# A two-layer decoder trunk on one core: smaller first weight load, norm sums closed before the operands, attention steps regrouped

## The chip, the cores and the metric

The kernel runs on one core of a Trainium2 chip. The metric is device time in microseconds (us) of one execution; three executions of the kernel before were timed, and one more was profiled. Engines: TensorE multiplies matrices (PE in the rows, PEld for its weight loads), VectorE (DVE) does two-operand arithmetic, ScalarE (ACT) functions and copies, GpSimd (POOL) almost nothing here, SyncE (SP) issues every load and store.

## The reference

Two layers over x of 256 positions x 1024 features, all float32. With adaLN columns shift, scale and gate made from c for each sub-layer, every sub-layer does x <- x + gate * f(rmsnorm(x) * (1 + scale) + shift):

```python
def reference(x, c, ...):
    sc = jax.nn.silu(c)
    for i in range(DEPTH):                      # DEPTH = 2
        mod = sc @ w_ada[i] + b_ada[i]
        sh_m, sc_m, g_m, sh_f, sc_f, g_f = jnp.split(mod, 6, axis=-1)
        h = modulate(x, norm_mix[i], sh_m, sc_m)
        y = moba_attention(h, ...) if i % 2 == 0 else short_conv(h, ...)
        x = x + g_m[:, None, :] * y
        h = modulate(x, norm_ffn[i], sh_f, sc_f)
        x = x + g_f[:, None, :] * swiglu(h, w_gate_up[i], w_down[i])
    return x
```

Layer 0 is attention with 8 heads of 128 features, RMS norm on q and k per head; with 256 positions there is one block of 256 keys, so it is plain causal attention. Layer 1 is a gated convolution of width 3. The channel mixer is SwiGLU with 2816 features.

## The kernel before, in words

**Numbers.** float32 products are made from two-part operands: a tile is split into a rounded part (`..h`, float32r) and the rest (`..l`), and `mm3` (line 250) issues three matmuls of 256 columns: high by high, high by low, low by high. The split costs one ScalarE copy and one VectorE subtraction for every tile (`prep` for weights, lines 91 to 100, each weight tile in two halves; `split` and others for activations).

**Order.** Up to the end of the first products (line 546 on, `manual_schedule`) TensorE, VectorE and ScalarE follow the written order. Behind it a scheduler lays out each engine's queue when the program is built: from the written order as priority, raised inside `high_priority(400)`, and from its own estimates of when an instruction could start. Once laid out, each engine takes its queue in order. SyncE's loads go in the written order. Weight tiles and the rows of the adaLN matrix share five buffers (`wf`), the split weights three (`wh`, `wl`); a load is issued when its buffer is free.

**Start (lines 546 to 621).** SyncE loads columns, x, the first adaLN pieces and `first_rows(0)`, the first 128 rows of the q and half of the k weights: 1536 columns, loaded as 1024 and then 512. The first norm's row factors are made, x is turned by TensorE, and for row block k = 0 to 7 the loop at line 594 makes the scale column (VectorE, `scale_column`), splits the weights (`w_operands` the first two of six 256-column pieces, `operands` the rest), makes the operand of the activations (`normed`, `h_operand`: `m0h` by ScalarE, `m0l` by VectorE) and issues `first_products`, six column tiles of six matmuls. For k = 0 all this stands above the loop: `shift_columns(y, 0)` (line 587), then `turn_x`, then `w_operands(0, wf)` (line 589), then `operands`. `keep_warm` issues matmuls whose result nobody reads.

**Attention (lines 624 to 762).** `tok_gemm` for the last two k tiles and four v tiles is the stream numbered g = 0 to 5, each of eight blocks k of six matmuls; g = 6 is the first group of `out_proj`, eight blocks of twelve. `plan[g, k]` names steps issued ahead of block k: `turn(j)` turns two k heads on TensorE and copies them out; `softmax(h)` makes the scores of head h, their maximum, exponential and normalisation; `turn_probs(h)` turns the probabilities; `mix_values(h)` multiplies them with v and splits the result into `ov` (line 725). In block k of g = 6 the output products read `ov[k]`. The plan of before places the four turns and the eight calls of each other step in four lists (lines 739 to 746).

**Norms (class `Norm`, lines 314 to 363).** `out_proj` finishes feature tiles of x in groups ([0, 1], [2], [3] of 256 features for the output projections, one each for the down projections), then for every tile of 128 calls `residual` (VectorE) and `done`. For the norms n0, n1, n2 `done` is `take(k)`: it squares the tile (ScalarE), adds the square to the running sum (VectorE; the last square is kept apart as `self.last`) and makes the two parts of the operand x * scale (`rh` by ScalarE, `rl` by VectorE). `raw_gemm` then starts the next matrix on x * scale without the row factor; at block k = 2 `rstd` (line 345) makes the mean square of each row by products of the sum, and of the last square, with the column `inv_d`, and at k = 4 `rows` turns the factors into a row tile. The result is multiplied by it at the end. In the last down projection `done` is `store`.

Of the kernel before, what the change touches and what calls it, by code (L numbers as in the profile page):

```python
# [33 lines left out]
def trunk_kernel(ctx: ExitStack, tc: tile.TileContext, x_t, cols_in, scale_in, shift_in, ada_in, qk_rows, kv_in, o_in,  # L34
# [99 lines left out]
    def first_rows(k):  # L134
        wf = wpool.tile([P, 8, CW], F32, tag="wf", name=f"wf_qk_{k}", bufs=5)
        flat = wf.rearrange("p k c -> p (k c)")
        for cs in (slice(0, D), slice(D, D + D // 2)):
            nc.sync.dma_start(flat[:, cs], qk_rows[k][:, cs])
        return wf

# [173 lines left out]
    class Norm:  # L314
# [2 lines left out]
        def __init__(self, name, l, sh, scl, raw):  # L317
            self.name, self.n, self.l, self.sh, self.scl, self.raw = name, 0, l, sh, scl, raw

        def take(self, k):  # L320
            sq = tmp.tile([P, S], F32, tag="sq", name=f"sq_{self.name}_{k}", bufs=2)
            nc.scalar.activation(sq, xT[:, k], AF.Square)
            if self.n == 0:
                self.sum = sq
            elif self.n == 1:
                s = tmp.tile([P, S], F32, tag="ssum", name=f"ss_{self.name}_{k}", bufs=1)
                nc.vector.tensor_add(s, self.sum, sq)
                self.sum = s
            elif self.n < KD - 1:
                nc.vector.tensor_add(self.sum, self.sum, sq)  # L330
            else:
                self.last = sq
            self.n += 1
            rh, rl = self.raw
            a = mcol(self.l, self.scl, k)
            nc.scalar.activation(rh[:, k, :S], xT[:, k], AF.Copy, scale=a)
            nc.vector.scalar_tensor_tensor(rl[:, k, :S], xT[:, k], a, rh[:, k, :S].bitcast(F32), op0=ALU.mult,
                                           op1=ALU.subtract)
            if k == (4 if self.sh == SH_F else 0):
                i = self.l * 48 + self.sh * KD  # L340
                sh = mod[:, i:i + KD].unsqueeze(2).to_broadcast([P, KD, 2])
                nc.scalar.activation(rh[:, :, S:], sh, AF.Copy)
                nc.vector.tensor_sub(rl[:, :, S:], sh, rh[:, :, S:].bitcast(F32))

        def rstd(self):
            ps = ps_misc("ms_" + self.name)
            for t in range(2):
                ts = slice(t * P, (t + 1) * P)
                nc.tensor.matmul(ps[:, t:t + 1], self.sum[:, ts], inv_d, start=True, stop=False)
                nc.tensor.matmul(ps[:, t:t + 1], self.last[:, ts], inv_d, start=False, stop=True)  # L350
            sd = tmp.tile([P, 2], F32, tag="sd", name="sd_" + self.name)
            r = tmp.tile([P, 2], F32, tag="rs", name="rs_" + self.name)
            with tc.high_priority(400):
                nc.scalar.activation(sd, ps[:, :2], AF.Sqrt, bias=eps)
                nc.vector.reciprocal(r, sd)
            self.r = r
# [8 lines left out]
    def residual(ps, l, gate, k):  # L365
        nc.vector.scalar_tensor_tensor(xT[:, k], ps, mcol(l, gate, k), xT[:, k], op0=ALU.mult, op1=ALU.add)

    def out_proj(keys, xs, l, gate, done, between={}):
        groups = [[0, 1], [2], [3]] if len(keys[0]) == 1 else [[j] for j in range(4)]
        for js in groups:  # L370
# [18 lines left out]
                        base + k == 0, base + k == total - 1)  # L389
                base += nk  # L390
            with tc.high_priority(400):
                for (j, o), ps in pss.items():
                    residual(ps, l, gate, 2 * j + o)
                    done(2 * j + o)

    def split(dst, k, src, name, psum_src=False):
        nc.scalar.activation(dst[0][:, k], src, AF.Copy)
# [133 lines left out]
    def keep_warm(n):  # L531

        ps = ps_misc("warm")
        for _ in range(n):
            nc.tensor.matmul(ps[:, :2 * P].rearrange("p (n c) -> p n c", c=P), ident_r,
                             ident_r.unsqueeze(1).to_broadcast([P, 2, P]), start=True, stop=True, skip_group_check=True)
# [9 lines left out]
    with tc.manual_schedule(engines={mybir.EngineType.PE, mybir.EngineType.DVE, mybir.EngineType.Activation}):  # L546
# [37 lines left out]
        t = normed(0)  # L584
        nc.vector.tensor_copy(xT[:, 2:4], x_ps)
        keep_warm(2)
        shift_columns(y, 0)
        x_ps = [turn_x(i, ps_alt) for i in (2, 3)]
        ops = w_operands(0, wf)
        operands(0, t, wf, ops)  # L590
        for i in range(2):
            nc.scalar.activation(xT[:, 4 + 2 * i:6 + 2 * i], x_ps[i], AF.Copy)
# [143 lines left out]
    for j in range(2):  # L736
        to_features(j, accs[4 + j])
    plan = {}
    for n, (g, k) in enumerate([[0, 4], [2, 4], [3, 1], [3, 7]]):
        plan.setdefault((g, k), []).append((turn, n))  # L740
    for n, (g, k) in enumerate([[3, 0], [3, 3], [3, 4], [4, 5], [5, 2], [5, 7], [6, 2], [6, 6]]):
        plan.setdefault((g, k), []).append((turn_probs, n))
    for n, (g, k) in enumerate([[2, 2], [2, 7], [3, 1], [3, 6], [4, 3], [5, 0], [5, 4], [5, 7]]):
        plan.setdefault((g, k), []).append((softmax, n))
    for n, (g, k) in enumerate([[3, 5], [3, 7], [4, 6], [5, 0], [5, 6], [6, 1], [6, 3], [6, 7]]):
        plan.setdefault((g, k), []).append((mix_values, n))

    def between(g):
        return {k: plan[g, k] for k in range(KD) if (g, k) in plan}
# [9 lines left out]

    av = new_pair("a", "a0", KF)  # L760
    n0 = Norm("n0", 0, SH_F, SC_F, raw_in(av))
    out_proj([[(("o", j), KD)] for j in range(4)], ov, 0, G_M, n0.take, between(6))
    zv, zraw = wide_pair("zv")
    n1 = Norm("n1", 1, SH_M, SC_M, zraw)
    ffn(0, n0, av, n1.take)


    ups = [act.tile([P, 2, S + 2], F32, tag=f"up{i}", name=f"up{i}") for i in range(2)]
# [33 lines left out]

    av = new_pair("a", "a1", KF)
    n2 = Norm("n2", 1, SH_F, SC_F, raw_in(av))
    out_proj([[(("co", j), KD)] for j in range(4)], zv, 1, G_M, n2.take)


    def store(k):
# [2 lines left out]
        elif k % 2:  # L811
            nc.sync.dma_start(out_f[:, k - 1:k + 1], xT[:, k - 1:k + 1])

    ffn(1, n2, av, store)


def _lay_out(inputs):
# [57 lines left out]
```

## Time and profile before

| | us |
|---|---|
| timed, median of 3 (lowest to highest) | 589.35 (589.28 to 589.84) |
| the profiled execution | 591.96 |
| its span, first to last instruction | 590.2 |
| TensorE busy in the span | 581.8 |
| VectorE busy | 453.3 |
| ScalarE busy | 315.1 |

Busy time of an engine says how much it did and not what the end waited for. A TensorE record is longer than the time that it takes from the next one, since matmuls overlap; the distance between two starts is the cost. A bracket behind a row of the timeline is idle time of that engine ahead of the instruction and what ended it. The chain that ended last is followed back from the last instruction, at each step to what released it.

### The profile page before, as it was taken

To read this page: it belongs to the slowest core of one execution; us is meant where nothing else is said; L and a number is where in the kernel's file an instruction comes from. 1 tells how busy PE (TensorE), PEld (TensorE's weight loads), DVE (VectorE), ACT (ScalarE), POOL (GpSimd) and SP (SyncE) were. 2 spreads that over 40 slices of the span, in tenths; PEclk is the share of its full clock that TensorE was granted. 3 is DMA by queue.
4 is the path that set the end of the run, shared out by engine and by line. 5 is a ranking of instruction groups with operands and counts; after the bars stand their busy time and mean duration, and the time that the engine had idled before them with its cause. 6 is when DMAs were issued, how large, how long until landed. Compare 5 with 4: busy or idle time off the path is not lost.

```text
span 590.2 us, 12039 instructions
## 1 busy us (share of the span) xinstructions
PE 581.8 (99%) x5044; PEld 573.0 (97%) x5044; DVE 453.3 (77%) x719; ACT 315.1 (53%) x526; POOL 1.1 (0%) x8
## 2 busy tenths in 40 slices
PE   8999999999999999999999999999999999999997
PEld 7999999999999999999999999999999999999997
DVE  4789898998989777868788999758976576565550
ACT  6457789596644353543337655446854454443330
POOL 0000000000000000000000000000000000000000
PEclk9999999999999999999999999999999999999999
DMA  8999998945898889768988279746386575655400
GB/s 322 396 378 406 354 330 318 349 159 205 323 344 329 325 314 355 261 219 330 338 339 300 87 284 366 267 143 230 132 351 243 190 284 189 242 183 191 160 18 18
DMA packets 25109, 156.04 MB, mean 264 GB/s; under 512 B 2784, under 2 KB 3168, under 8 KB 8928
## 3 DMA queue, kind: packets, MB, share of 16 engines
q1 hardware_dynamic: 25056, 155.28, 71.0%
q8 instruction: 39, 0.64, 0.4%
q14 instruction: 14, 0.11, 0.0%
HBM read 154.22 MB, written 1.05 MB: 263 GB/s over the span
## 4 chain that ended last, share of the span: by engine, by line
PE 86%; DMA 5%; DVE 5%; ACT 2%; issue 1%; SPq 0%; DVEq 0%; ACTq 0%
PE pu L252 7%; PE pu L253 7%; PE pu L256 7%; PE pg L252 6%; PE pg L256 6%; PE pg L253 6%; DMA wa<-in_ada_dram 4%; PE op_d L256 4%; PE op_d L253 4%; PE op_d L252 4%; PE pq L252 1%; PE pq L253 1%; PE op_o L252 1%; PE raw_f L252 1%; DVE prod L109 1%
## 5 line engine op out<-in xcount | busy, mean ns | idle before, releaser
L109 DVE SCALAR_TENSOR_TENSOR prod<-wa,c_all 128x1024 f32<-128x1024 f32 x80 | 97.7, 1221 | 26.9 <-DMA wa<-in_ada_dram 26.0
L99 DVE TENSOR_TENSOR wl_d<-wf_d,wh_d 128x1024 fp32r<-128x1024 f32 (+1 forms) x48 | 52.9, 1132 | 23.7 <-ACT wh_d L98 23.7
L98 ACT ACTIVATE wh_d<-wf_d 128x1024 fp32r<-128x1024 f32 (+1 forms) x48 | 44.8, 979 | 44.5 <-PE op_d L253 22.3
L98 ACT ACTIVATE wh_g<-wf_g 128x1024 fp32r<-128x1024 f32 x44 | 45.8, 1052 | 41.9 <-issue 41.7
L99 DVE TENSOR_TENSOR wl_u<-wf_u,wh_u 128x1024 fp32r<-128x1024 f32 x44 | 52.3, 1220 | 13.3 <-ACT wh_u L98 13.1
L98 ACT ACTIVATE wh_u<-wf_u 128x1024 fp32r<-128x1024 f32 x44 | 44.6, 1050 | 32.7 <-issue 27.1
L99 DVE TENSOR_TENSOR wl_g<-wf_g,wh_g 128x1024 fp32r<-128x1024 f32 x44 | 53.4, 1221 | 1.7 <-ACT wh_g L98 1.6
L256 PE MATMUL op_d<-a0h,wl_d 128*128 128x256 f32 x176 | 49.1, 279 | 1.1 <-DVE wl_d L99 1.1
L252 PE MATMUL op_d<-a0h,wh_d 128*128 128x256 f32 x176 | 48.8, 277 | 0.0
L253 PE MATMUL op_d<-a0l,wh_d 128*128 128x256 f32 x176 | 48.8, 277 | 0.0
L252 PE MATMUL op_d<-a1h,wh_d 128*128 128x256 f32 x176 | 48.6, 276 | 0.0
L253 PE MATMUL op_d<-a1l,wh_d 128*128 128x256 f32 x176 | 48.6, 276 | 0.0
L256 PE MATMUL op_d<-a1h,wl_d 128*128 128x256 f32 x176 | 48.6, 276 | 0.0
L252 PE MATMUL pg<-f0h,wh_g 128*128 128x256 f32 x160 | 44.5, 278 | 0.0
L256 PE MATMUL pg<-f0h,wl_g 128*128 128x256 f32 (+3 forms) x164 | 44.4, 275 | 0.0
L252 PE MATMUL pg<-f1h,wh_g 128*128 128x256 f32 x160 | 44.2, 277 | 0.0
L253 PE MATMUL pg<-f0l,wh_g 128*128 128x256 f32 x160 | 44.2, 276 | 0.0
L252 PE MATMUL pu<-f0h,wh_u 128*128 128x256 f32 x160 | 44.2, 276 | 0.0
L253 PE MATMUL pu<-f0l,wh_u 128*128 128x256 f32 x160 | 44.2, 276 | 0.0
L256 PE MATMUL pu<-f0h,wl_u 128*128 128x256 f32 x160 | 44.2, 276 | 0.0
L253 PE MATMUL pg<-f1l,wh_g 128*128 128x256 f32 x160 | 44.2, 276 | 0.0
L256 PE MATMUL pg<-f1h,wl_g 128*128 128x256 f32 x160 | 44.2, 276 | 0.0
(296 smaller groups left out, 2027.6 us busy)
## 6 DMA issues: line engine op xcount, KB each, us to landing
wa<-in_ada_dram SPq DMA_DIRECT2D x40, 1024.0 KB, 6.0
wf_g<-in_gate_up_dram SPq DMA_DIRECT2D x22, 1024.0 KB, 5.1
wf_u<-in_gate_up_dram SPq DMA_DIRECT2D x22, 1024.0 KB, 5.0
wf_d<-in_down_dram SPq DMA_DIRECT2D x16, 1024.0 KB, 6.9
wf_d<-in_down_dram SPq DMA_DIRECT2D x8, 768.0 KB, 4.9
wa_sc<-in_scale_dram SPq DMA_DIRECT2D x8, 512.0 KB, 6.6
wa_sh<-in_shift_dram SPq DMA_DIRECT2D x8, 512.0 KB, 7.5
wf_qk<-in_qk_rows_dram SPq DMA_DIRECT2D x8, 512.0 KB, 6.4
```

What stands on the lines that cost most here:

```text
L98: nc.scalar.activation(wh[:, a:b], wf[:, a:b], AF.Copy)
L99: nc.vector.tensor_sub(wl[:, a:b], wf[:, a:b], wh[:, a:b].bitcast(F32))
L109: nc.vector.scalar_tensor_tensor(t, w, 1.0, c_all, op0=ALU.mult, op1=ALU.mult, accum_out=dst)
L252: nc.tensor.matmul(ps, ah, bh, start=first, stop=False, skip_group_check=True)
L253: nc.tensor.matmul(ps, ah, bl, start=False, stop=False, skip_group_check=True)
L256: nc.tensor.matmul(ps[:, a:b], al, bh[:, a:b], start=False, stop=last, skip_group_check=True)
```

## The change

1. `first_rows`: the first row block's weights are loaded as 512 and then 1024 columns; the other seven as before. `w_operands(0, wf)`, the split of the first 512 columns, is written ahead of `shift_columns(y, 0)`.
2. `Norm.take` becomes `square` and `operand`. The last square is added to the sum as well, and `rstd` makes two products with `inv_d` where it made four. `out_proj` calls, for each tile of x, residual, square, operand as before; in the group of the last tiles it makes both residuals, then both squares, then both operands. The stores of the last projection come behind both residuals in the same way.
3. The plan of attention has eleven stops and the first `turn`. At stop i stand, where they exist, `mix_values(i - 3)`, `turn_probs(i - 2)`, `turn(i + 1)` and `softmax(i)`.

```diff
--- before.py
+++ after.py
@@ -134,7 +134,9 @@
     def first_rows(k):
         wf = wpool.tile([P, 8, CW], F32, tag="wf", name=f"wf_qk_{k}", bufs=5)
         flat = wf.rearrange("p k c -> p (k c)")
-        for cs in (slice(0, D), slice(D, D + D // 2)):
+
+        n = D if k else D // 2
+        for cs in (slice(0, n), slice(n, D + D // 2)):
             nc.sync.dma_start(flat[:, cs], qk_rows[k][:, cs])
         return wf
 
@@ -317,7 +319,7 @@
         def __init__(self, name, l, sh, scl, raw):
             self.name, self.n, self.l, self.sh, self.scl, self.raw = name, 0, l, sh, scl, raw
 
-        def take(self, k):
+        def square(self, k):
             sq = tmp.tile([P, S], F32, tag="sq", name=f"sq_{self.name}_{k}", bufs=2)
             nc.scalar.activation(sq, xT[:, k], AF.Square)
             if self.n == 0:
@@ -326,11 +328,11 @@
                 s = tmp.tile([P, S], F32, tag="ssum", name=f"ss_{self.name}_{k}", bufs=1)
                 nc.vector.tensor_add(s, self.sum, sq)
                 self.sum = s
-            elif self.n < KD - 1:
+            else:
                 nc.vector.tensor_add(self.sum, self.sum, sq)
-            else:
-                self.last = sq
             self.n += 1
+
+        def operand(self, k):
             rh, rl = self.raw
             a = mcol(self.l, self.scl, k)
             nc.scalar.activation(rh[:, k, :S], xT[:, k], AF.Copy, scale=a)
@@ -346,8 +348,7 @@
             ps = ps_misc("ms_" + self.name)
             for t in range(2):
                 ts = slice(t * P, (t + 1) * P)
-                nc.tensor.matmul(ps[:, t:t + 1], self.sum[:, ts], inv_d, start=True, stop=False)
-                nc.tensor.matmul(ps[:, t:t + 1], self.last[:, ts], inv_d, start=False, stop=True)
+                nc.tensor.matmul(ps[:, t:t + 1], self.sum[:, ts], inv_d, start=True, stop=True)
             sd = tmp.tile([P, 2], F32, tag="sd", name="sd_" + self.name)
             r = tmp.tile([P, 2], F32, tag="rs", name="rs_" + self.name)
             with tc.high_priority(400):
@@ -389,9 +390,16 @@
                         base + k == 0, base + k == total - 1)
                 base += nk
             with tc.high_priority(400):
-                for (j, o), ps in pss.items():
-                    residual(ps, l, gate, 2 * j + o)
-                    done(2 * j + o)
+
+                ks = [[2 * j + o] for j, o in pss]
+                ks = [sum(ks, [])] if js[0] == 3 else ks
+                pss = {2 * j + o: ps for (j, o), ps in pss.items()}
+                for group in ks:
+                    for k in group:
+                        residual(pss[k], l, gate, k)
+                    for fn in done:
+                        for k in group:
+                            fn(k)
 
     def split(dst, k, src, name, psum_src=False):
         nc.scalar.activation(dst[0][:, k], src, AF.Copy)
@@ -584,9 +592,9 @@
         t = normed(0)
         nc.vector.tensor_copy(xT[:, 2:4], x_ps)
         keep_warm(2)
+        ops = w_operands(0, wf)
         shift_columns(y, 0)
         x_ps = [turn_x(i, ps_alt) for i in (2, 3)]
-        ops = w_operands(0, wf)
         operands(0, t, wf, ops)
         for i in range(2):
             nc.scalar.activation(xT[:, 4 + 2 * i:6 + 2 * i], x_ps[i], AF.Copy)
@@ -736,14 +744,12 @@
     for j in range(2):
         to_features(j, accs[4 + j])
     plan = {}
-    for n, (g, k) in enumerate([[0, 4], [2, 4], [3, 1], [3, 7]]):
-        plan.setdefault((g, k), []).append((turn, n))
-    for n, (g, k) in enumerate([[3, 0], [3, 3], [3, 4], [4, 5], [5, 2], [5, 7], [6, 2], [6, 6]]):
-        plan.setdefault((g, k), []).append((turn_probs, n))
-    for n, (g, k) in enumerate([[2, 2], [2, 7], [3, 1], [3, 6], [4, 3], [5, 0], [5, 4], [5, 7]]):
-        plan.setdefault((g, k), []).append((softmax, n))
-    for n, (g, k) in enumerate([[3, 5], [3, 7], [4, 6], [5, 0], [5, 6], [6, 1], [6, 3], [6, 7]]):
-        plan.setdefault((g, k), []).append((mix_values, n))
+
+    points = [[2, 2], [2, 6], [3, 2], [3, 6], [4, 2], [4, 6], [5, 2], [5, 5], [6, 0], [6, 3], [6, 5]]
+    plan[0, 4] = [(turn, 0)]
+    for i, at in enumerate(points):
+        plan[tuple(at)] = [(fn, n) for fn, n, ok in ((mix_values, i - 3, 0 <= i - 3), (turn_probs, i - 2, 0 <= i - 2 < 8),
+                                                     (turn, i + 1, i < 3), (softmax, i, i < 8)) if ok]
 
     def between(g):
         return {k: plan[g, k] for k in range(KD) if (g, k) in plan}
@@ -759,10 +765,10 @@
 
     av = new_pair("a", "a0", KF)
     n0 = Norm("n0", 0, SH_F, SC_F, raw_in(av))
-    out_proj([[(("o", j), KD)] for j in range(4)], ov, 0, G_M, n0.take, between(6))
+    out_proj([[(("o", j), KD)] for j in range(4)], ov, 0, G_M, (n0.square, n0.operand), between(6))
     zv, zraw = wide_pair("zv")
     n1 = Norm("n1", 1, SH_M, SC_M, zraw)
-    ffn(0, n0, av, n1.take)
+    ffn(0, n0, av, (n1.square, n1.operand))
 
 
     ups = [act.tile([P, 2, S + 2], F32, tag=f"up{i}", name=f"up{i}") for i in range(2)]
@@ -802,7 +808,7 @@
 
     av = new_pair("a", "a1", KF)
     n2 = Norm("n2", 1, SH_F, SC_F, raw_in(av))
-    out_proj([[(("co", j), KD)] for j in range(4)], zv, 1, G_M, n2.take)
+    out_proj([[(("co", j), KD)] for j in range(4)], zv, 1, G_M, (n2.square, n2.operand))
 
 
     def store(k):
@@ -811,7 +817,7 @@
         elif k % 2:
             nc.sync.dma_start(out_f[:, k - 1:k + 1], xT[:, k - 1:k + 1])
 
-    ffn(1, n2, av, store)
+    ffn(1, n2, av, (store,))
 
 
 def _lay_out(inputs):
```

## Rows read from the trace of the kernel before

**Rows 1.** The profile's page: busy time, share of the span and instructions of each engine; the TensorE clock granted in 40 equal slices of the span (tenths of full speed, 9 is 90% or more); shares of the chain of work that ended last, by engine.

```profile
PE 581.8 (99%) x5044; PEld 573.0 (97%) x5044; DVE 453.3 (77%) x719; ACT 315.1 (53%) x526; POOL 1.1 (0%) x8
...
PEclk9999999999999999999999999999999999999999
...
PE 86%; DMA 5%; DVE 5%; ACT 2%; issue 1%; SPq 0%; DVEq 0%; ACTq 0%
```

**Rows 2.** The view of waits, TensorE's own, whole span: who waited for whom, us in total, times, the longest in us.

```profile
PE op_d L256 <- DVE wl_d L99: 1.1, 2, 0.6
PE pv L253 <- DVE wl_v L99: 0.6, 1, 0.6
PE op_o L252 <- ACT ovh L397: 0.5, 1, 0.5
```

**Rows 3.** The timeline from 11.8 to 14 us: start us, us, engine, line, operation, out<-in, shapes, count, and in brackets the idle time of the engine before it and what ended it.

```profile
11.83 0.26 ACT L479 ACTIVATE mod<-mod_c_sh,cols 128x1 f32<-128x1 f32 x1 [0.63 <-PE mod_c_sh L473]
...
11.99 0.62 ACT L503 ACTIVATE wh_qk<-wf_qk 128x512 fp32r<-128x512 f32 x1
...
12.48 0.72 PE L535 MATMUL warm<-ident_r 128*128 128x256 f32 x4
...
12.51 0.50 ACT L497 ACTIVATE m0h<-t_m,mod 128x256 fp32r<-128x256 f32 x1
...
12.65 0.69 DVE L504 TENSOR_TENSOR wl_qk<-wf_qk,wh_qk 128x512 fp32r<-128x512 f32 x1 [0.91 <-ACT wh_qk L503]
...
13.06 0.39 PE L252 MATMUL pq<-m0h,wh_qk 128*128 128x256 f32 x1
...
13.26 0.48 DVE L498 SCALAR_TENSOR_TENSOR m0l<-t_m,mod,m0h 128x256 fp32r<-128x256 f32 x1
...
13.79 0.39 PE L253 MATMUL pq<-m0l,wh_qk 128*128 128x256 f32 x1 [0.34 <-DVE m0l L498]
```

**Rows 4.** Windows: busy us (and instructions) of TensorE, its weight loads, VectorE, ScalarE and GpSimd in a stretch, then the granted clock, the DMA engines' share and GB/s.

```profile
20.00:25.00 5.00, 5.00 (x51) 4.39 (x45) 3.38 (x7) 2.33 (x7) 0.00 (x0) 1.00 1.04 406
...
57.00:118.00 61.00, 59.78 (x479) 57.51 (x478) 55.06 (x113) 48.02 (x137) 0.00 (x0) 1.00 0.92 340
```

**Rows 5.** The timeline from 22 to 25.2 us, ScalarE, VectorE and TensorE, columns as in rows 3: row block 2 of the first products.

```profile
22.14 0.63 ACT L503 ACTIVATE wh_qk<-wf_qk 128x512 fp32r<-128x512 f32 x1 [0.76 <-DMA wf_qk<-in_qk_rows_dram]
...
24.53 0.49 DVE L498 SCALAR_TENSOR_TENSOR m0l<-t_m,mod,m0h 128x256 fp32r<-128x256 f32 x1 [0.64 <-ACT m0h L497]
...
24.79 0.28 PE L256 MATMUL pk<-wh_qk,m0l 128*128 128x256 f32 x1
24.90 0.28 PE L252 MATMUL pq<-m0h,wh_qk 128*128 128x256 f32 x1
25.07 0.38 PE L253 MATMUL pq<-m0l,wh_qk 128*128 128x256 f32 x1
```

**Rows 6.** TensorE's timeline, 133.1 to 134 us: the products with `inv_d` of norm n0 and the next product.

```profile
133.16 0.28 PE L349 MATMUL ms_n<-inv_d,ss_n 128*128 128x1 f32 x2
133.30 0.36 PE L350 MATMUL ms_n<-inv_d,sq_n 128*128 128x1 f32 x2
133.52 0.36 PE L349 MATMUL ms_n<-inv_d,ss_n 128*128 128x1 f32 x2
133.74 0.36 PE L350 MATMUL ms_n<-inv_d,sq_n 128*128 128x1 f32 x2
133.97 0.36 PE L252 MATMUL raw_f<-a0h,wh_g 128*128 128x258 f32 x1
```

**Rows 7.** The timeline of ScalarE, VectorE and TensorE around the last square of each norm (n0 at 132, n1 at 318, n2 at 407 us).

```profile
132.24 1.22 DVE L99 TENSOR_TENSOR wl_u<-wf_u,wh_u 128x1024 fp32r<-128x1024 f32 x1
...
132.35 0.42 ACT L322 ACTIVATE sq_n<-xT 128x256 f32<-128x256 f32 x1
...
317.65 0.40 ACT L322 ACTIVATE sq_n<-xT 128x256 f32<-128x256 f32 x1
...
318.10 0.38 PE L350 MATMUL ms_n<-inv_d,sq_n 128*128 128x1 f32 x2
...
406.89 1.22 DVE L99 TENSOR_TENSOR wl_u<-wf_u,wh_u 128x1024 fp32r<-128x1024 f32 x1
...
408.16 0.28 PE L349 MATMUL ms_n<-inv_d,ss_n 128*128 128x1 f32 x2
```

**Rows 8.** The timeline of ScalarE and TensorE in the attention stretch, 71 to 118 us.

```profile
71.56 1.14 ACT L675 ACTIVATE tk<-pk,rk 128x128 f32<-128x128 f32 x4 [2.49 <-PE pt L683]
...
91.57 2.00 ACT L98 ACTIVATE wh_v<-wf_v 128x1024 fp32r<-128x1024 f32 x2
...
93.47 0.79 ACT L708 ACTIVATE pr<-pr,rsm 128x128 f32<-128x128 f32 x2
...
93.93 0.39 PE L253 MATMUL pv<-wl_v,m0h 128*128 128x256 f32 x1 [0.64 <-DVE wl_v L99]
...
116.98 0.38 ACT L397 ACTIVATE ovh<-po 128x256 fp32r<-128x256 f32 x1 [1.58 <-PE po L724]
...
117.42 0.74 PE L252 MATMUL op_o<-ovh,wh_o 128*128 128x256 f32 x4 [0.47 <-ACT ovh L397]
```

**Rows 9.** The timeline of SyncE's queue at the end of the span: the last two stores.

```profile
585.33 2.37 SPq L810 DMA_DIRECT2D out_dram<-xT  x2
```

**Rows 10.** The chain that ended last, in order of time (start us, us, what): the scores of the head whose probabilities are normalised at 93.47 in rows 8.

```profile
80.69 0.32 PE s L689 x2
```

## The prediction

> **What bounds the kernel now.** I read the page first. TensorE is busy 99% of the span at the full granted clock, and 86% of the chain that ended last is TensorE [rows 1]. So time can only come from TensorE's own instructions, or from the few places where it stands still. The view of waits says how little that is: 1.1 us in two waits on `op_d`, 0.6 us on `pv`, 0.5 us on `op_o` [rows 2], and the start. For each of the three parts of the change I then read the stretch in which it lies and asked what is late next. A gain of TensorE counts only up to the next place where it would wait for something that has not moved.
>
> The profiled execution took 591.96 us, of which its span is 590.2; 1.8 us lie around it. The median of the three timed runs is 589.35, which is 2.6 us less. I work out differences on the profiled execution and take them from the median.
>
> **First weights split ahead of the shift.** The number of loads and bytes stays (256 KB then 512 KB, instead of 512 then 256). One ScalarE and one VectorE instruction move ahead of `shift_columns`. Before, ScalarE makes the shift at 11.83, splits the weights at 11.99 and makes `m0h` at 12.51; VectorE's `wl_qk` at 12.65 then holds `m0l` until 13.26, and TensorE's second product waits for it until 13.79 [rows 3]. After, the split fits into the 0.63 us for which ScalarE stood idle ahead of the shift: its first 256 KB are there by 11.99 less 256 KB / 406 GB/s = 0.63 us, so 11.36 at the latest [rows 3, 4], and the split takes 0.52 us start to start (11.99 to 12.51). If the load were late, the shift and `m0h` would queue behind it on ScalarE; that margin excludes it. Then `m0h` starts about 12.0, `m0l` about 12.5 (when `m0h` is written) instead of 13.26, and the second product 0.53 us behind it as before, about 13.07: 0.7 us earlier. The first product gains only 0.13, since the four warm-up matmuls from 12.48 keep TensorE until some 12.93.
>
> I cost this part at nothing all the same. At row block 2 ScalarE waits 0.76 us for the load of `wf_qk` and starts at 22.14; from there the chain runs `wh_qk`, `wl_qk`, t, `m0h`, `m0l` (24.53) to TensorE's product at 25.07, which starts 0.17 us after the one before it where that one took 0.11, so it already waits a little for `m0l` [rows 5]. In that stretch the DMA engines are at a share of 1.04 and 406 GB/s [rows 4]. No byte less is moved ahead of that load, so it lands when it landed, `m0l` is ready when it was, and TensorE meets it at 25.07 in both kernels. From there on nothing has moved. So 0.7 us are won at 13.8 and given back by 25.07. Bounds: 0.7 won if the loads were to land earlier too, nothing lost; I take 0.
>
> **Last square summed ahead.** In each of the three norms two of the four products with `inv_d` go (line 350). Each shows as a pair of records, since the rows say x2, and the four groups start at 133.16, 133.30, 133.52 and 133.74, the next product at 133.97 [rows 6]: 0.22 us for each product with a one-column moving operand. Two fewer give 0.44 us, three norms 1.3 us. All of it lies on TensorE in stretches where it has no waits. VectorE gets one more addition of some 0.4 us per norm, off the path as long as it is done when TensorE comes. That is the new wait: before, TensorE needed the last square straight from ScalarE; now it needs the sum behind it on VectorE. In n1 the square (317.65, 0.40 us) ended just as TensorE took it at 318.10 [rows 7]. There both residuals are now made before the squares, so the last square moves up by about the 0.4 us of an addition and more; I expect no loss. In n0 the square of 132.35 ends at 132.77, but VectorE took a weight split of 1.22 us at 132.24; if the addition queues behind it, it is done at about 133.46 + 0.4 = 133.85, where TensorE wants it at 133.16: 0.7 us waited. In n2 the same: split at 406.89 to 408.11, sum at some 408.5, wanted at 408.16: 0.35 us [rows 7]. The two residuals next to each other and the priority of the squares let the addition come before these splits, so I take no loss; bounds for the part: 1.3 won to 1.3 - 0.7 - 0.35 = 0.25 won. Lower down nothing absorbs the gain: in the down projection of layer 0 VectorE, not TensorE, is late at the two waits on `wl_d` [rows 2], but the loads and splits there are released by work that itself follows TensorE's weight tiles from the gate and up products on, and moves with it. No single row shows that whole; if it is not so, what the third part and n0 win (0.5 + 0.44) ends there, which the range holds. In the other groups `square` and `operand` come in the order of the old `take`, so nothing moves there. The operands of the last two blocks come some 0.4 us later, and are wanted four blocks of 12 products x 0.115 us = 5.5 us after the norm's products: covered.
>
> The Trainium skill has a rule against the size of this part. Its page TensorE: Matmul & The Clock Gate, section Back-to-back issue gap, lists some 25 ns as the gap of a matmul with 1 to 64 columns; by that twelve dropped records would give 0.3 us and not 1.3. The rows above show 0.11 us a record, so the measurement decides; the rule stays among the rivals.
>
> **Steps at eleven stops.** Every step of attention is still done once; only its place in the stream of `pk`, `pv` and first output products changes, so the sum of TensorE's work stays. What can change is the two waits. (a) Before, the last `mix_values` stands directly ahead of block 7, which reads its result; TensorE waits for `ovh` (ScalarE 116.98) until 117.42, idle 0.47 us [rows 8]. After, it stands two blocks ahead, 24 products x 0.115 = 2.8 us, where the copy and the difference take some 0.8 us. I count this 0.5 us as won. (b) `pv` waits 0.64 us at 93.93 for the split of the last v weights, which ScalarE began only at 91.57 [rows 8], because its queue stood on earlier steps. After, `turn(1)` comes two blocks earlier, and it is `turn(1)` that kept ScalarE idle 2.49 us ahead of the `tk` of 71.56 [rows 8]. That should bring the splits forward, but the order on ScalarE is the scheduler's, so I count nothing and keep 0.6 for the range. Against it: VectorE is busy 55.1 of the 61 us from 57 to 118 [rows 4], so a step that queues badly there costs a split or an adaLN product of 1.2 us. Bounds for the part: 1.1 won to 0.6 lost (half of one such instruction); I take 0.5 won.
>
> **The end.** The two last stores (585.33, both issued by 587.70 [rows 9]) now stand behind both residuals in the program. Each should still wait for its own residual alone: 0, at worst 0.4 us if the first waits for the second and the issues follow each other.
>
> Sum: 0 - 1.3 - 0.5 = 1.8 us less: 589.35 - 1.8 = 587.5 (590.2 - 1.8 = 588.4 for the span of a profiled execution like this one).
>
> **Rivals.**
> 1. The first part is not absorbed: 587.5 - 0.7 = 586.8. For it: only the bandwidth argument; against it: the product at 25.07.
> 2. The added sums come late (the wait that takes the place of the removed products): the second part gives 0.25, the third nothing: 589.1. For it: the splits of 132.24 and 406.89. Against it: the scheduler can put TensorE's products of the norm later, since other products are at hand.
> 3. Slower. TensorE takes `turn_probs` two stops after `softmax`, 8 blocks x 6 x 0.115 = 5.5 us plus the steps of two stops, about 3 us. Before, one head's scores stood at 80.69 [rows 10] and were normalised at 93.47 [rows 8], 12.8 us later, because VectorE and ScalarE were full. If TensorE's order is fixed as written and two or three heads are that late, each costs up to 12.8 - 8.5 = 4 us less what the others catch up, say 3.5 in all: 589.35 - 1.3 + 3.5 = 591.5. It decides once a head needs over 8.5 us from scores to normalised. Against it: before, too, the steps ran later than written without a wait.
> 4. The third part changes nothing (the scheduler's order meets the same two waits): 589.35 - 1.3 = 588.05, on the border.
> 5. The removed records cost 0.025 us each and not 0.11 (the rule of the Trainium skill above): 589.35 - 0.3 - 0.5 = 588.5.
>
> **How the numbers follow.** Forecast 0.56; rivals 0.05, 0.15, 0.09, 0.12 and 0.03. A measurement here tells from no change about 0.2%, 1.2 us: faster means under 588.2, slower over 590.5. Faster: 0.56 + 0.05 + half of rival 4 = 0.67; same: 0.15 + 0.06 + 0.03 = 0.24; slower 0.09. The range: low 589.35 - 1.3 - 1.1 - 1.1 (both `pv` and `op_o` waits, and the two `op_d` waits, should a shifted order clear them) = 585.8; high 589.35 - 0.25 + 0.6 = 589.7, which leaves out rival 3.
>
> **What would show it.** Part one: the second product about 13.1 instead of 13.79, and a wait of TensorE near 25.0 that ends at the same 25.07; if TensorE reaches `q_sums` 0.7 us earlier, I was wrong. Part two: two `ms_n` groups per norm, 0.44 us less from the first to the next product, and no wait of TensorE on `ss_n`. Part three: no wait of `op_o` on `ovh`, and `pv` on `wl_v` shorter or gone. A new wait of TensorE on `pr`, `prt` or `ss_n` would make the prediction wrong.

## The result and the profile after

The kernel after takes **586.42 us** (median; 586.28 to 586.60), the kernel before 589.55 (589.28 to 589.84): ratio 0.9947, 95% interval [0.9935, 0.9958], 3.1 us less. The forecast was 587.5, in a range of 585.8 to 589.7.

The page and TensorE's waits of the kernel after, which answer to [rows 1] and [rows 2]:

```profile
span 584.8 us, 12020 instructions
...
PE 577.4 (99%) x5032; PEld 569.8 (97%) x5032; DVE 454.8 (78%) x722; ACT 316.1 (54%) x526; POOL 1.1 (0%) x8
...
PE 93%; DMA 2%; DVE 2%; ACT 1%; issue 1%; SPq 0%; ACTq 0%; DVEq 0%
```

```profile
PE warm L543 <- DVE ident_r L555: 1.8, 1, 1.8
PE xT L551 <- ACT c_all L578: 1.0, 1, 1.0
PE ms_n L351 <- DVE ss_n L332: 0.4, 1, 0.4
PE mod_ps_sh L469 <- DMA wa_sh<-in_shift_dram: 0.3, 1, 0.3
PE mod_ps_sc L469 <- DMA wa_sc<-in_scale_dram: 0.3, 1, 0.3
```

Twelve of TensorE's records are gone (5044 to 5032: two products of two records in each of three norms). All the waits of [rows 2] are gone too, and behind the start one is new, `ms_n` on `ss_n`; the other four stand in the first 20 us. TensorE's share of the chain, 93% where [rows 1] have 86%, is no gain of the change: a second profile of the kernel before, told below, has 93% as well.

Where the time went is read best by cutting the span at the same instructions of TensorE in each trace. The lengths below (us) are differences of start times. "Again" is a second profile of the kernel before, and A, B and C are the three parts alone; all four are told in the next section.

| stretch | before | again | A | B | C | after | after less again |
|---|---|---|---|---|---|---|---|
| start to `q_sums` | 53.56 | 53.74 | 53.82 | 53.75 | 53.75 | 53.62 | -0.12 |
| to the last `op_o` (attention) | 76.61 | 76.70 | 76.77 | 76.74 | 74.70 | 74.69 | **-2.01** |
| to `settle_f` (n0) | 12.71 | 12.69 | 12.70 | 12.31 | 12.68 | 12.32 | **-0.37** |
| to the first `op_d` | 109.59 | 109.59 | 109.59 | 109.59 | 109.59 | 109.59 | 0 |
| to the last `op_d` of layer 0 | 62.40 | 59.73 | 59.73 | 59.73 | 59.72 | 59.73 | 0 |
| to the last `raw_m` (n1) | 12.73 | 12.58 | 12.57 | 12.81 | 12.58 | 12.81 | **+0.23** |
| to the last `op_co` | 77.57 | 77.43 | 77.57 | 77.42 | 77.56 | 77.41 | -0.02 |
| to the last `raw_f` of layer 1 (n2) | 12.57 | 12.60 | 12.57 | 12.19 | 12.57 | 12.20 | **-0.40** |
| to the end | 172.44 | 172.44 | 172.43 | 172.44 | 172.44 | 172.43 | 0 |
| span | 590.18 | 587.50 | 587.75 | 586.98 | 585.59 | 584.80 | -2.70 |

The start alone differs by up to 0.8 us between profiles of kernels whose code there is the same (53.4 to 54.2 in the traces of this study), so differences in the other rows say more than the whole span does. Of the 78 executions of the kernel before that were timed beside the experiments, seven took more than 591 us, about as long as its first profiled one (591.96).

**The first part** did what was forecast. The timeline of the kernel after, around the first products and at row block 2, answers to [rows 3] and [rows 5]:

```profile
11.10 0.62 ACT L511 ACTIVATE wh_qk<-wf_qk 128x512 fp32r<-128x512 f32 x1
...
12.67 0.48 DVE L506 SCALAR_TENSOR_TENSOR m0l<-t_m,mod,m0h 128x256 fp32r<-128x256 f32 x1 [0.23 <-ACT m0h L505]
...
13.04 0.28 PE L254 MATMUL pq<-m0h,wh_qk 128*128 128x256 f32 x1
...
13.21 0.39 PE L255 MATMUL pq<-m0l,wh_qk 128*128 128x256 f32 x1
...
22.21 0.63 ACT L511 ACTIVATE wh_qk<-wf_qk 128x512 fp32r<-128x512 f32 x1 [0.93 <-DMA wf_qk<-in_qk_rows_dram]
...
24.81 0.28 PE L254 MATMUL pq<-m0h,wh_qk 128*128 128x256 f32 x1
25.14 0.39 PE L255 MATMUL pq<-m0l,wh_qk 128*128 128x256 f32 x1
```

The second product comes at 13.21 instead of 13.79. At row block 2 ScalarE stands longer for the same load (0.93 instead of 0.76 us), the split starts at 22.21 (before: 22.14), and TensorE now waits visibly, from 24.81 to 25.14, where it was at 25.07 before. All that was won has gone again.

**The second part**, in n0, answers to [rows 6]: from the first product with `inv_d` to the next product 0.44 us instead of 0.81.

```profile
130.03 1.22 DVE L99 TENSOR_TENSOR wl_u<-wf_u,wh_u 128x1024 fp32r<-128x1024 f32 x1
130.43 0.40 ACT L324 ACTIVATE sq_n<-xT 128x256 f32<-128x256 f32 x1
...
131.16 0.42 DVE L332 TENSOR_TENSOR ss_n<-ss_n,sq_n 128x256 f32<-128x256 f32 x1
...
131.66 0.58 PE L351 MATMUL ms_n<-inv_d,ss_n 128*128 128x1 f32 x4
132.10 0.37 PE L254 MATMUL raw_f<-a0h,wh_g 128*128 128x258 f32 x1
```

The last sum came behind a weight split (130.03) here too and was done at 131.58, 0.08 us before TensorE's products. In n2 it is the same: split at 401.88, sum from 403.02 to 403.44, products at 403.51.

**The third part.** From [rows 8], the split of the last v weights now begins at 90.44 instead of 91.57, and the last `po` stands two blocks ahead of its reader, so that `ovh` is made while other products run:

```profile
90.44 1.99 ACT L98 ACTIVATE wh_v<-wf_v 128x1024 fp32r<-128x1024 f32 x2
...
112.43 0.39 PE L732 MATMUL po<-vp 128*128 128x128 f32 x2
...
112.57 0.36 PE L254 MATMUL op_o<-ovh,wh_o 128*128 128x256 f32 x1
...
112.85 0.38 ACT L405 ACTIVATE ovh<-po 128x256 fp32r<-128x256 f32 x1 [2.99 <-PE po L732]
```

**The stores** at the end go as before ([rows 9]): one row of two, from 579.95, and the last stretch of the table is the same to 0.01 us.

### The profile page after: what moved, and what is told of

It reads as the page before. It is cut to its first block, busy times and chain, and to the rows that moved or that the text cites. A ratio compares the mean times of both kernels' runs of the same rounds, so it can differ in the third digit from the quotient of the medians.

```text
span 584.8 us, 12020 instructions
## 1 busy us (share of the span) xinstructions
PE 577.4 (99%) x5032; PEld 569.8 (97%) x5032; DVE 454.8 (78%) x722; ACT 316.1 (54%) x526; POOL 1.1 (0%) x8
## 4 chain that ended last, share of the span: by engine, by line
PE 93%; DMA 2%; DVE 2%; ACT 1%; issue 1%; SPq 0%; ACTq 0%; DVEq 0%
PE pu L255 7%; PE pu L254 7%; PE pu L258 7%; PE op_d L255 6%; PE op_d L254 6%; PE op_d L258 6%; PE pg L254 6%; PE pg L258 6%; PE pg L255 6%; PE raw_f L254 1%; PE op_o L258 1%; PE raw_f L255 1%; PE raw_f L258 1%; PE pb L258 1%; PE pb L254 1%; PE op_o L254 1%
## 5 line engine op out<-in xcount | busy, mean ns | idle before, releaser
L258 PE MATMUL pu<-f1h,wl_u 128*128 128x256 f32 x160 | 44.2, 276 | 0.0
```

The costliest lines, as they stand in the source:

```text
L258: nc.tensor.matmul(ps[:, a:b], al, bh[:, a:b], start=False, stop=last, skip_group_check=True)
```

## The experiments

**The kernel before, once more.** No edit. 

> The kernel before, unchanged, profiled a second time. The profiled execution of before took 591.96 us, 2.6 over its timed median, and it alone shows the two waits of op_d on wl_d (1.1 us in the view of waits) with 235 products behind them at 117.8 ns instead of 113.3 (some 1.0 us more). Theory one, the op_d waits are a matter of that one execution: a second profile takes about 589.5, without them, and from the first op_d to the last it takes some 59.7 us as in the kernel after, instead of 62.4. Theory two, they belong to the kernel: the second profile shows them again and takes about 592, and the timed 589.5 has to come from somewhere else.

It took 589.27 us, span 587.5. `op_d` on `wl_d` is not among its waits; `pv` on `wl_v` (0.6) and `op_o` on `ovh` (0.5) are. The windows from the first to the last `op_d`, of the first and then of the second profile (busy time and instructions of TensorE, granted clock, DMA share, GB/s):

```profile
252.50:314.90 62.40, 61.25 (x530) 1.00 0.81 305
```

```profile
252.70:312.50 59.80, 59.80 (x530) 1.00 0.84 314
```

The same 530 records in 2.6 us less at the same clock: the first theory. The two waits of `op_d` and the slower products behind them belong to that execution and not to every one of the kernel. Whether the few others of its length have them too, no trace shows. The medians don't hold them, so the change did not win them.

**The first part alone.** The edits at `first_rows` and at `ops = w_operands(0, wf)`. 

> Before with the first part alone: the first 512 weight columns come by themselves and are split ahead of the shift. Prediction: the second product starts 0.7 us earlier, the product of row block 2 at the same 25.1, and the time stays (0.0, less than 0.3 either way). Rival (first part not absorbed): 0.7 us less, 588.85.

589.51 us, ratio 0.9997 [0.9984, 1.001]; `q_sums` at 53.82 against 53.74. The interval alone (0.9 us less to 0.6 us more) would still hold the 0.7 us of rival 1. The traces speak against it: in the seven with the new start and no other change of the loads, the second product comes at 13.38 in the mean against 13.79 in the six with the old one, the first product with `m0l` of row block 2 at 25.18 against 25.25, and `q_sums` at 53.81 against 53.75. As forecast: nothing.

**The second part alone.** `square`, `operand`, the two products less and the grouping in `out_proj`. 

> Before with the second part alone: last squares added ahead, two products less per norm. By the prediction 1.3 us less (0.44 in each of three norms, no wait on the sum). By the reading of the trace of after: 0.4 in n0 and in n2 and nothing in n1, where TensorE waits 0.4 us for the sum, so 0.8 us less. If the removed records were worth 25 ns each: 0.2 less or even some time more, with the wait of n1.

588.97 us, ratio 0.9992 [0.9973, 1.0012]: by the times alone no difference. Its stretches are plain, though: n0 0.38 and n2 0.41 us shorter, n1 0.23 longer, the rest the same: 0.55 us less. That is the second reading. n1 is dealt with below.

**The third part alone.** The plan of eleven points. 

> Before with the third part alone: the steps of attention at eleven stops. By the prediction 0.5 us less (the wait of op_o alone). By the reading of the trace of after: 1.9 us less, since the wait of op_o (0.47), the wait of pv (0.64) and the slower pace of the products behind them (about 118 instead of 113 ns, some 190 products, 0.8 us) go together. Rival: with the scheduler's order elsewhere unchanged, the op_d waits stay and 0.5 to 1.9 is all that is seen.

587.44 us, ratio 0.9960 [0.9947, 0.9973]; all of it in the attention stretch, 76.70 to 74.70 us. So the third part is the bulk of the gain, four times what was forecast for it. My explanation by pace does not hold: TensorE's products go at one of two paces (about 113 or 118 ns start to start; see the experiment on odd-sized products), and behind the stops more of them go at the slower one than before, about four in five against somewhat over half. That costs some 0.4 to 0.5 us.

**The last head earlier.** On the kernel before, in the lists of `turn_probs` and `mix_values`:

```
-[..., [6, 2], [6, 6]]            +[..., [6, 2], [6, 5]]
-[..., [6, 1], [6, 3], [6, 7]]    +[..., [6, 1], [6, 3], [6, 6]]
```

> Before, with the turning of the last head's probabilities one block of products earlier and its last mix_values with it, and nothing else moved. Theory: the wait of op_o on ovh goes, and with it the whole excess of the last stop (1.41 us in the second profile of before against 0.69 for such a stop elsewhere): 0.7 us less than before, 588.85. By the prediction's term 0.5 less, 589.05. Rival: the heads' queue on ScalarE and VectorE was what made it late, so that turn_probs or op_o waits instead: 589.55.

588.67 us, ratio 0.9983 [0.9971, 0.9994]; the attention stretch is 75.94 us, 0.76 less. Its TensorE goes from the last `po` into `op_o` with no wait, while `ovh` is still being made:

```profile
115.27 0.38 PE L724 MATMUL po<-vp 128*128 128x128 f32 x2
...
115.41 0.36 PE L252 MATMUL op_o<-ovh,wh_o 128*128 128x256 f32 x1
...
115.69 0.39 ACT L397 ACTIVATE ovh<-po 128x256 fp32r<-128x256 f32 x1 [1.58 <-PE po L724]
```

The wait had cost 0.7 us and not the 0.47 that stands in brackets in [rows 8]. From the product ahead of the stop to the product behind it, start to start, such a stop takes 0.69 us here and 1.41 in the second profile of before. The bracket counts only the time with nothing in TensorE's pipeline.

**The turns earlier.** On the kernel before, in the list of `turn`:

```
-[[0, 4], [2, 4], [3, 1], [3, 7]]    +[[0, 4], [2, 2], [2, 6], [3, 2]]
```

> Before, with the turning of the key heads alone where the change puts it (turn 1 to 3 at the places 2.2, 2.6 and 3.2 instead of 2.4, 3.1 and 3.7). Theory: this is what takes away the wait of pv on wl_v (0.71 us over a normal row) and the long stop of s at 79.7 (0.45 over a normal one), so 1.1 us less than before: 588.45, and together with the 0.8 of the last head it makes up the 2.0 of the third part. By the prediction, which counted nothing here: 589.55. Rival: the softmax and mix_values that the change moves as well are needed: less than 0.4 less.

588.67 us, ratio 0.9992 [0.9983, 1.0001]. The times alone don't settle it; the attention stretch is 75.58 us, 1.12 less than 76.70, as the theory has it. Ahead of the `tk` of [rows 8] ScalarE stands 0.33 us instead of 2.49, and starts it at 69.96, 1.8 us earlier than in the second profile of before:

```profile
69.96 1.14 ACT L675 ACTIVATE tk<-pk,rk 128x128 f32<-128x128 f32 x4 [0.33 <-PE pt L683]
```

and TensorE's waits no longer name `pv`, nor `s` on `qkT` (0.2 in the second profile of before, 0.45 us start to start); `op_o` on `ovh` stays:

```profile
PE warm L535 <- DVE ident_r L547: 1.8, 1, 1.8
PE op_o L252 <- ACT ovh L397: 0.5, 1, 0.5
PE pq L253 <- DVE m0l L498: 0.3, 1, 0.3
```

1.12 and 0.76 make 1.88 of the 2.01 us of the third part. If they add up, the softmax places that the change moved too are hardly needed for it; no run has both edits together, so that they add up is not shown.

**The steps spread out.** On the kernel after, `turn_probs` one block ahead of its stop, `mix_values` two blocks ahead (but for the last), `turn` one behind:

```
+for i, (g, k) in enumerate(points):
+    if 0 <= i - 3: put(g, k, 2 if i < 10 else 0, mix_values, i - 3)
+    if 0 <= i - 2 < 8: put(g, k, 1, turn_probs, i - 2)
+    if i < 8: put(g, k, 0, softmax, i)
+    if i < 3: put(g, k, -1, turn, i + 1)
```

> After, with the steps of attention at the same distances but not together: at most of the eleven stops turn_probs comes a block ahead and mix_values two blocks ahead of softmax, so that TensorE's products are interrupted 27 times instead of 18 (22 in the kernel before). The last mix_values stays. Theory one, an interruption itself costs about 0.1 us (the trace shows some 35 ns between two steps and a product of 0.20 instead of 0.11 us behind a stop): 0.8 to 1.0 us more than after, 587.3. Theory two, only the waits counted: as after, 586.4, or a new wait of po on the copied probabilities, which the trace would name.

588.02 us, ratio to before 0.9985 [0.9971, 0.9999]; the attention stretch is 75.94 us, 1.25 more than after. The size looks like theory one, but the trace speaks for theory two:

```profile
79.05 0.49 PE L697 MATMUL s<-qkT 128*128 128x128 f32 x2 [0.28 <-ACT pr L712]
...
97.90 0.14 PEld L723 LDWEIGHTS prt<-ident,pr 128*128 128x128 f32 x1 [0.31 <-ACT pr L716]
```

The stop at 79.05 takes 1.43 us start to start where a softmax alone takes 0.89, and the weight load of the `prt` of 97.90 stood 0.31 us for ScalarE's `pr`. And my 0.1 us an interruption was counted wrongly: a turn (0.47) and a softmax (0.89) apart hold two products of 0.11, together (1.33) one. With the slower product behind the turn (0.09) both ways come to the same within 0.02 us. Stops are not worth merging for their number; the distances between steps are what counts. How the 1.25 us divide over the new waits I did not settle.

**All row blocks loaded in the new way.** On the kernel after, `n = D // 2` for every `k`. 

> After, with the first 512 weight columns loaded by themselves in all eight row blocks and not in the first alone. Theory (the gain of the first part is taken back at row block 2, whose first load lands too late): those 256 KB land 0.63 us earlier there, the product at 25.14 starts some 0.3 to 0.6 us earlier, and the time is up to 0.5 us less than after: 586.0. Rival: another input of row block 2 (the scale columns' weights or the shift) is nearly as late, or the later, larger load holds up the columns 512 to 1023 instead: 586.4 or slower.

587.93 us, ratio to before 0.9980 [0.9962, 0.9998]; its executions lie anywhere from 586.66 to 591.72, and the profiled one (586.77) is among the shortest. In that one the theory is seen at work:

```profile
21.32 0.63 ACT L511 ACTIVATE wh_qk<-wf_qk 128x512 fp32r<-128x512 f32 x1 [0.33 <-DMA wf_qk<-in_qk_rows_dram]
...
24.50 0.28 PE L254 MATMUL pq<-m0h,wh_qk 128*128 128x256 f32 x1
24.61 0.28 PE L255 MATMUL pq<-m0l,wh_qk 128*128 128x256 f32 x1
```

The split starts 0.9 us earlier (21.32 against 22.21), the wait at the second product is gone, and `q_sums` comes at 52.99 instead of 53.62. In the seven traces with the new load in the first block alone, this product with `m0l` comes no earlier than 24.92 and `q_sums` no earlier than 53.43. So it was that load that took the first part's gain back. But of these 0.63 us nothing is left at the last `op_o`: the attention stretch is 0.93 us longer (75.62), and TensorE arrives there later than after did. Why the longer executions are longer is open; no trace of one was taken.

**n1 one block later.** On the kernel after, in `raw_gemm`:

```
+late = name == "m1"
-if k == 2:        +if k == 2 + late:      (norm.rstd)
-if k == 4:        +if k == 4 + late:      (norm.rows)
```

> After, with the norm n1 alone taken by TensorE one block of 12 products later (and its row of reciprocals one block later too). Theory: in n1 the last sum queues behind a weight split of 1.23 us on VectorE, and TensorE stands 0.57 us for it; one block later (1.43 us) it is there. Then no wait of TensorE on ss_n, and 0.6 us less than after: 585.8. Rival: n1 is not late because of the place of the products but because its operands come later, so that the wait moves to the first products with the normalised operands: 586.4, as after.

**585.89 us** (585.3 to 586.12), ratio to before 0.9936 [0.9924, 0.9948]: the lowest median of the study, though this interval overlaps that of after. The stretch of n1 says it clearly: 12.11 us instead of 12.81, and no wait of TensorE on `ss_n`. First VectorE, the last square on ScalarE and TensorE's products in n1 of the kernel after, then the same products a block later:

```profile
309.49 0.47 DVE L367 SCALAR_TENSOR_TENSOR xT<-op_d,mod,xT 128x256 f32<-128x256 f32 x1
310.51 0.42 DVE L332 TENSOR_TENSOR ss_n<-ss_n,sq_n 128x256 f32<-128x256 f32 x1 [0.54 <-ACT sq_n L324]
310.85 0.48 DVE L367 SCALAR_TENSOR_TENSOR xT<-op_d,mod,xT 128x256 f32<-128x256 f32 x1
311.25 0.48 DVE L339 SCALAR_TENSOR_TENSOR zvl<-xT,mod,zvh 128x256 fp32r<-128x256 f32 x1
311.73 0.40 ACT L324 ACTIVATE sq_n<-xT 128x256 f32<-128x256 f32 x1
311.86 1.23 DVE L99 TENSOR_TENSOR wl_cb<-wf_cb,wh_cb 128x1024 fp32r<-128x1024 f32 x1
313.00 0.42 DVE L332 TENSOR_TENSOR ss_n<-ss_n,sq_n 128x256 f32<-128x256 f32 x1
...
313.47 0.61 PE L351 MATMUL ms_n<-inv_d,ss_n 128*128 128x1 f32 x4 [0.40 <-DVE ss_n L332]
```

```profile
312.79 0.42 DVE L332 TENSOR_TENSOR ss_n<-ss_n,sq_n 128x256 f32<-128x256 f32 x1
...
313.98 0.28 PE L258 MATMUL raw_m<-zvh,wl_cu 128*128 128x258 f32 x1
314.10 0.50 PE L351 MATMUL ms_n<-inv_d,ss_n 128*128 128x1 f32 x4
```

Read VectorE's column of starts: residual, sum, residual, operand, split, sum. The last square was made at 311.73 to 312.13, but at 311.86 VectorE had taken a split of 1.23 us, and the sum came behind it at 313.00. A block later the sum is long done (313.21, products at 314.10), and from the first product with `inv_d` to the next product it takes 0.36 us.

**The odd-sized products left out.** On the kernel after, one line in `ffn`:

```
-feat_gemm([(pg, ...)], hs, KD, (128, 64, 192, 96) if (l, j) == (0, 1) else ())
+feat_gemm([(pg, ...)], hs, KD, ())
```

> After, with the four odd-sized products of the first gate chunk of layer 0 made whole (the same columns in one product instead of two each); the ones at pb stay. Theory: TensorE's pace (113.3 or about 117.8 ns from start to start of a product of 256 columns) changes only at an interruption, and those four are what brings it from 117.8 to 113.3 there; without them the 1462 products up to the next norm go at 117.8: 6.5 us more, 592.9. Rival: the pace belongs to the stretch, or comes back by itself: 586.4 or 0.1 less.

592.59 us, ratio to before 1.0053 [1.0038, 1.0067], 6.2 us over after. Two windows of TensorE, first of after and then of this kernel:

```profile
160.00:240.00 80.00, 80.00 (x708) 1.00 0.91 337
250.00:300.00 50.00, 50.00 (x444) 1.00 0.80 294
```

```profile
160.00:240.00 80.00, 80.00 (x682) 1.00 0.89 337
250.00:300.00 50.00, 50.00 (x427) 1.00 0.82 311
```

80 us / 708 = 113.0 ns and 80 us / 682 = 117.3 ns a product, at the same granted clock, with no wait in either, and from 250 us on it is still so. (A window also counts the products that it cuts at its ends; start to start it is 113.3 and 117.8 ns.) The pace theory holds.

**Odd-sized products behind the last stop.** On the kernel with n1 late, in `out_proj`:

```
+cuts = [128, 64, 192, 96] if between else []
-    base + k == 0, base + k == total - 1)
+    base + k == 0, base + k == total - 1, cuts.pop(0) if cuts and k >= 6 and o else 0)
```

> The kernel with n1 taken a block later, and four odd-sized products of the same kind behind the last stop of attention, in the first output products. Theory of the pace: the products from there to the end of the output projection (some 110) go at 113.3 instead of 117.8 ns, 0.4 to 0.5 us less than with n1 alone: 585.4. Rival: which pace follows an interruption is a matter of the instant at which it falls, and these may not hit it: 585.9, as without them.

586.76 us, ratio to before 0.9953 [0.9941, 0.9965]. The pace did change to 113.3 ns at 117.7 us. But n0 became 0.85 us longer (13.32 instead of 12.47):

```profile
130.68 1.21 DVE L99 TENSOR_TENSOR wl_u<-wf_u,wh_u 128x1024 fp32r<-128x1024 f32 x1
131.82 0.42 DVE L332 TENSOR_TENSOR ss_n<-ss_n,sq_n 128x256 f32<-128x256 f32 x1
...
132.29 0.61 PE L351 MATMUL ms_n<-inv_d,ss_n 128*128 128x1 f32 x4 [0.76 <-DVE ss_n L332]
```

It is n1's mechanism again, now in n0, where the prediction had looked for it: the sum behind a split. In the kernel after, the same order in n0 had left 0.08 us to spare.

**The same with n0 late too.** `late = name != "f1"`. 

> The kernel of the run before last (n1 a block later, four odd-sized products behind the last stop), with the norm n0 taken a block later as well. In that run the pace behind the odd-sized products did change to 113.3 ns, and TensorE then stood 0.76 us in n0 for a sum that queued behind a weight split of 1.21 us on VectorE. Theory: n0 a block later takes this wait away and what the pace gives shows: 0.9 to 1.0 us less than the run with the wait, and 0.1 to 0.3 less than with n1 alone: 585.7. Rival: in n0 the operands that follow are late then (the wait moves to the first products of the next gate chunk): 586.8, as with the wait.

586.24 us (585.59 to 587.17), ratio to before 0.9942 [0.9926, 0.9958]. The wait in n0 is gone (12.25 us). From `q_sums` to the end it takes 530.23 us against 530.45 with n1 late alone, the 0.2 less that was hoped for; in the times the two can't be told apart.

## Why the prediction was right, and where not

**The bound.** Right: no work of TensorE went but the twelve records, and what else was won are its waits.

**The profiled execution against the median.** I took differences on an execution that lay 2.6 us over the median and left open why. It was the two waits on `op_d` and the pace behind them, which the second profile does not have. They were counted into the low end of my range (585.8), and had no place there. Without them the range would have begun at 586.9, and the measured 586.4 lies below that: that it fell inside is luck.

**First part: 0, measured 0.** By each step: the split in ScalarE's gap, the second product earlier (13.21; I had said about 13.1), the load of row block 2 that takes it back. The experiment on the loads shows that it was this load.

**Second part: 1.3 won, measured 0.55.** The price was right: 0.37 to 0.41 us in n0 and n2 for 0.44 forecast. What is missing goes with the sum's coming just in time. In the traces of this study the four records take 0.36 to 0.40 us where the sum was done 0.15 us or more before them (0.45 less than the 0.81 of before at best), and 0.42 to 0.47 where it was done 0.1 us or less before them. By the 25 ns of the Trainium skill (page TensorE: Matmul & The Clock Gate, section Back-to-back issue gap) the four records would have been 0.1 us; the trace has about 0.1 us for each, so the measurement decides again, and that rival falls.

The step that failed is "There both residuals are now made before the squares, so the last square moves up by about the 0.4 us of an addition and more; I expect no loss" (in n1). VectorE's order there is residual, sum, residual, as it was in the kernel before; `out_proj` lists both residuals first, but the scheduler put the first sum between them. In the second profile of the kernel before:

```profile
311.99 0.48 DVE L366 SCALAR_TENSOR_TENSOR xT<-op_d,mod,xT 128x256 f32<-128x256 f32 x1
313.01 0.42 DVE L330 TENSOR_TENSOR ss_n<-ss_n,sq_n 128x256 f32<-128x256 f32 x1 [0.54 <-ACT sq_n L322]
313.36 0.48 DVE L366 SCALAR_TENSOR_TENSOR xT<-op_d,mod,xT 128x256 f32<-128x256 f32 x1
```

The last square was not earlier, and the sum fell behind a split: -0.44 became +0.23. I had described this very mechanism, as rival 2, for n0 and n2, and took no loss from it in any of the three norms. In n0 and n2 the sum fell behind a split too, so my reason there, that the priority of the squares lets the addition come before the splits, was wrong as well. The last square did come 0.3 to 0.4 us earlier against TensorE there (its end 0.83 us before the products in n0, where [rows 6] and [rows 7] have 0.39), and the sum was done 0.08 us in time. That nothing was waited for in these two rests on that margin, which is luck: in the run with odd-sized products behind the last stop n0 did wait 0.76 us.

**Third part: 0.5 won, measured 2.0.** The direction and the named waits were right, and the size was off in two terms. The wait of `op_o` was put at its bracket, 0.47; taken away alone it gave 0.76. The wait of `pv` was counted at nothing; with the turns alone it went, together with a shorter stall of a softmax, for 1.12. Both waits, at their brackets, had made the part's bound of 1.1 won, and 2.0 lies beyond it.

**Stores: 0, measured 0.** **Rival 3** (heads late, slower) did not come: no wait on `pr` or `prt`. The kernel with the steps spread out shows what it would have looked like: 1.6 us more.

In the profiles the sum is 0 - 0.55 - 2.0 = -2.55, against -2.70 from the second profile of before to after; the rest is the start. The medians differ by 3.1; the interval of the ratio (2.5 to 3.8 us less) holds the 2.7. The forecast of -1.8 was too small because the third part's error (1.5) outweighed the second's (0.75) the other way.

## What to carry to other kernels

Where one engine is busy all the time, price a wait by the start-to-start distance of the work on its two sides against the same place without it, not by its idle time alone; and profile a kernel twice before a wait of the profile is taken for the kernel's. When a sum moves to an engine that also takes long, unrelated instructions, read the order in which that engine will take them: one instruction of 1.2 us that slips ahead takes nearly three times what the dropped products save. And moving the consumer by a block can be the cheapest cure.

## What the hardware showed unexpectedly

TensorE's products of 256 columns go at one of two paces, 113.3 or 117.8 ns start to start, both at a granted clock of 1.00. In every trace of this study a pace lasts until something interrupts the stream and then stays, over 1400 products and more. The interruptions are waits, products of another kind, products of odd size, and in a few places a product or two of 0.15 to 0.24 us for which the view of waits names nothing (289.45 in the first profile of before). The four odd-sized products at the start of layer 0's gate chunks ended at 113.3 in every trace that had them; without them 117.8 stayed for 1488 products, 175 us. So an interruption can cost 4.5 ns times the products that follow it: in the first profile of before, two waits with 1.1 us idle made 2.67 us. What in the chip holds the pace was not tried.
